# New h scaled sixteen rows behind its result, operand sums and row scales at other rows, and one more pair whose weights are added by POOL

## The chip, the cores and the metric

The kernel runs on one core of one Trainium2 chip. The metric is the device time of one execution, in microseconds. The core has five engines that each work through their own list of instructions in order: PE (matmuls), ACT and DVE (work on whole tiles of 128 partitions), POOL, and SP, which issues most transfers. POOL issues transfers too, among them those that add to what lies in the destination.

## The reference

Two layers over a hidden state h of 512 tokens by 2048 channels. Layer 0 is a hybrid of forgetting attention and an RWKV-7 time mix; layer 1 is a gated MLP with spatial gating. After each layer h is updated twice: once by the normed output of the layer, and once by a gated product of the per-layer inputs p. All is fp32. What matters here is the end of layer 0 and the beginning of layer 1:

```
for i in range(DEPTH):
    xn = rms_norm(h, norm_pre[i])
    ...                                   # layer 0: attention and time mix; layer 1:
    proj = xn @ c_w_in[j]
    u, v, g = _split(proj, (GMLP_W, GMLP_W, GMLP_W))
    oc = chunked_spatial_gating(u, v, c_ln_g[j], c_ln_b[j], c_w_s[j], c_b_s[j])
    y = (oc * jax.nn.silu(g)) @ c_w_out[j]
    ...
    h = h + rms_norm(y, norm_post[i])
    h = h + (p[i] @ ple_w_proj[i]) * jax.nn.sigmoid(h @ ple_w_gate[i])
```

The last line of layer 0 is the stage called the gate here (`first_gate`), and `xn @ c_w_in` of layer 1 is `layer_c`. The norm of layer 1 is split in two: the column factor `norm_pre` is multiplied onto the new h (line 1164), and the row factor, one over the root of the mean square of each token, comes later, from sums of squares.

## The kernel before, in words

**Products.** Each fp32 number is written as a high and a low part, and each product takes three matmuls (high by high, high by low, low by high). The large products, 512 by 2048 by 2048 and the like, are made by a Strassen-Winograd scheme: seven products of half size in place of eight, for a pair of column blocks of the weight. A `Pair` stands for 512 + 512 columns; `seven` (line 1547) runs the products in the order handed in. In the gate and in the first third of layer_c that order is for two pairs, a and b: b1 a1 b2 a2 a5 a6 a3 a4 a7 b5 b6 b3 b4 b7. The letters V, U and G of layer_c are the three thirds of `c_w_in`; its first product stage is over V[0] (a) and V[1] (b).

**Rows.** Each of the products has eight rows, one for each 128 input channels of the half. A row is one cast of a weight tile to its high part on ACT (line 1541, into `whi`), one subtraction on DVE that makes the low part (line 1542, `wlo`), and then PE's matmuls: 12 of 256 columns in the gate, 6 of 512 columns in layer_c. `whi` and `wlo` have four buffers each, so ACT and DVE can be four rows ahead of PE. If a pair is `whole`, each fifth row of weights uses a pair of extra buffers, `half0` and `half1`; otherwise those buffers take half tiles of the load for product 4.

**Weights.** Each product needs a sum or difference of weight blocks. Products 1, 2, 3 and 6 load blocks over SP's queue. Products 5 and 7 add a block by an accumulate transfer that POOL issues (`grow`, line 1489). Product 6 adds two tiles on DVE (line 1493). Product 4 depends on the pair: a `whole` pair adds by POOL's transfer, another loads two half tiles over SP's queue and adds each on DVE, again at line 1493.

**Operands.** The other side of each product, h, also enters as sums and differences of its quarters. In the names of the program `yh`, `xh`, `xl`, `yl`, `sq`, `sg` are tiles of 128 by 512 for such sums and their parts; a sum is made on DVE (lines 1413 and 1414), its high part by ACT (line 973), its low part by DVE (line 974). The steps `s1`, `s24`, `s3`, `x2`, `x22` make the operands of product 5 (s1), of 6 and 3 (s24), of 7 (s3) and of 2 and 4 (x2, x22); each has four parts q. `early(q)` copies a quarter of h as the operand of product 1 of the next stage.

**What sets the order.** `later(n, step)` notes a step n rows ahead; `tick` counts a row and runs the steps that are due (line 1469). The order on an engine then follows from the priority of an instruction, the place where it was written, and `high_priority`, which puts instructions ahead of others written earlier; a scheduler that builds the program fixes each engine's list from that. While it runs, nothing passes anything else on one engine.

**A result of the gate.** `emit` (lines 1142 to 1168) takes one result: a sigmoid on ACT, a multiplication and the addition to h on DVE (lines 1152 to 1154), the square on ACT (line 1155) and, on DVE, its sum into `accq` or `rstdB` (line 1157, which of them depends on the half e of the tokens). Line 1159 stores the new h from the `yh` tile over SP's queue to `hd` in DRAM, and the scale of line 1164 writes `yh` times `norm_pre` over the same tile, in two ACT instructions of 128 by 256. The scale has to wait until the store has read the tile. In the kernel before it is noted five rows behind the result. After the last product `self.clock += 100` runs all steps left over.

**Row factors.** `done` (line 1733) is called after each product of layer_c; after the first one it puts 16 matmuls with a tile of ones against `accq` and `rstdB` (line 1739), which add up the squares of each token and give the row factors.

Of the kernel before, what the change touches and what calls it, by code (L numbers as in the profile page):

```python
# [11 lines left out]
AF = mybir.ActivationFunctionType  # L12
# [4 lines left out]
P = 128  # L17
# [89 lines left out]
class Net:  # L107
# [986 lines left out]
    def first_gate(self, H, state, wp, ps):  # L1094
        nc, i = self.nc, self.i
        s, update, s1, s24, s3, x22 = state
        npre = self.cols["norm_pre"]
# [5 lines left out]
        def late(q):  # L1103
            update(q, 1)
            update(q + 4, 1)
            s1(q)

        def fetch(tiles, *which):
# [18 lines left out]
        cs, x2 = C[0], C[2]  # L1127

        def early(q):
            if q == 0:  # L1130
                cs[1] = self.whole_set()
            self.put(cs[1], q, H[q, 0])

        steps = [((1, 6, 19, 28)[q], lambda q=q: late(q)) for q in range(4)]
        steps += [((11, 15, 33, 37)[q], lambda q=q: s24(q)) for q in range(4)]
        steps += [((23, 26, 43, 45)[q], lambda q=q: s3(q)) for q in range(4)]
# [5 lines left out]
        steps += [(90, lambda: fetch([self.slot("xl", k, F32) for k in range(4)], (6, 1), (7, 1), (4, 1), (5, 1)))]  # L1142
        steps += [(103 + q, lambda q=q: x2(q)) for q in range(4)]
        steps += [(107 + q, lambda q=q: early(q)) for q in range(4)]
        for n, step in sorted(steps, key=lambda x: x[0]):
            self.later(n, step)

        def emit(pr, m, n, src):
# [12 lines left out]
            def scaled():  # L1161
                for a in range(2):
                    c = 16 + 2 * q + a
                    nc.scalar.activation(H[q, e][:, a, :], H[q, e][:, a, :], AF.Copy, scale=npre[:, c : c + 1])

            self.later(5, scaled)

        W = i["ple_w_gate"][0]
        self.seven(FIRST(*[Pair(W, 2 * j * T, 2 * j, emit) for j in range(2)]), Sets(s), ps, fm=True)
        self.clock += 100  # L1170
        self.tick()
        s1, s24, s3, x22 = C[3:]
        steps = [(2 + 3 * q, lambda q=q: s1(q)) for q in range(4)]
        steps += [(14 + 4 * q, lambda q=q: s24(q)) for q in range(4)]
        steps += [(30 + 2 * q, lambda q=q: s3(q)) for q in range(4)]
        steps += [(38 + 2 * q, lambda q=q: x22(q, True)) for q in range(4)]
        return accq, last["act"], cs, steps
# [435 lines left out]
    def layer_c(self, cp, sets, steps, accq, after, wp, ps):  # L1613
# [83 lines left out]
        G = [Pair(W, 2 * D + 2 * j * T, 2 * j, silu) for j in range(2)]  # L1697
        for pr in V:
            pr.whole = False
        order = FIRST(*V)  # L1700
# [32 lines left out]
        def done(step):  # L1733
            if step == 0:
                pc = self.t(ps, [P, 4, 2], "mm")
                for m in range(4):
                    for a in range(2):
                        c = 256 * a + m % 2 * P
                        nc.tensor.matmul(
                            pc[:, m, :], accq[m // 2][:, c : c + P], self.ones[:, 0:2], start=(a == 0), stop=(a == 1)  # L1740
                        )
                self.row_rstd(pc, rc, after)
                bs = self.t(wp, [P, T], "sq")[0:KT, 0:P]
                nc.sync.dma_start(bs, i["c_b_s"][0])

                def turned():
                    pt = self.t(ps, [P, KT], "mm")
                    nc.tensor.transpose(pt, bs, self.ident[0:KT, 0:KT])
                    self.bsT = self.t(lp, [P, KT], "bsT")
                    nc.vector.tensor_copy(self.bsT, pt)  # L1750

                self.later(12, turned)
# [290 lines left out]
```

## Time and profile before

| | |
|---|---|
| median of 3 runs | 2242.57 us (2239.11 to 2243.87) |
| profiled execution | 2242.89 us, span 2241.2 us, mean granted clock 0.994 |
| casts of the gate | from 1175.6 us of the span |
| casts of layer_c | from 1375.2 us |
| scales of line 1164 | 1242.1 to 1409.1 us |
| adds of half tiles, line 1493 | 1442.7 to 1516.9 us |

Times inside the span are counted from its start. A row of the timeline gives the start, the length, the engine, the line, the operation and its tiles, and in brackets how long the engine had nothing to run before and what released it. A row of the windows gives for each engine the busy time in the window and, in brackets, its instructions, then the granted clock of PE (1.00 is full speed), the busy share of the DMA engines and the data rate.

### The profile page before, as it was taken

What the parts mean: (1) busy time and instruction counts of PE and PEld (TensorE: products, weight loads), DVE (VectorE), ACT (ScalarE), POOL (GpSimd) and SP (SyncE); (2) the same over time, 40 slices, a digit from 0 to 9 for tenths busy, and PEclk for the clock granted to TensorE, in tenths of its full rate; (3) what the DMA queues carried; (4) which work ended last, traced back from release to release, by engine and by line L of the source; (5) the groups of instructions that cost most, each with busy time, mean ns of one, the idle gap of its engine ahead of it and who ended that gap; (6) DMA issues with size and microseconds to landing.
All of it is one profiled execution on the core that took longest, in us unless ns stands there. A gap on an engine that the chain in (4) does not pass through costs nothing. (4 is left out here: it accounts for less than half of the span.)

```text
span 2241.2 us, 43473 instructions
## 1 busy us (share of the span) xinstructions
PE 2193.2 (98%) x16535; PEld 1879.1 (84%) x16535; DVE 1666.0 (74%) x3236; ACT 1352.8 (60%) x2764; POOL 295.2 (13%) x356
## 2 busy tenths in 40 slices
PE   8999999999999999999999999999999999999998
PEld 7878888888888788889999998777877878999887
DVE  8766667666634777787879867887677678978977
ACT  5545545555543677766567656655565567757754
POOL 2000010101000000000210111011121121120031
PEclk9999999999999999999999999999999999999999
DMA  7322222223223633326988878589779687688796
GB/s 236 92 79 67 77 77 79 79 68 86 77 81 101 212 94 104 99 80 199 197 228 234 185 188 205 155 200 224 163 158 238 160 194 179 148 198 264 212 239 170
DMA packets 304208, 343.35 MB, mean 153 GB/s; under 512 B 15821, under 2 KB 188014, under 8 KB 302974
## 3 DMA queue, kind: packets, MB, share of 16 engines
q1 hardware_dynamic: 238590, 243.03, 34.8%
q0 software_dynamic: 43520, 83.90, 21.8%
q10 hardware_dynamic: 21888, 13.64, 2.2%
q8 instruction: 130, 2.13, 0.4%
q14 instruction: 80, 0.66, 0.1%
HBM read 305.61 MB, written 34.90 MB: 152 GB/s over the span
## 5 line engine op out<-in xcount | busy, mean ns | idle before, releaser
L1542 DVE TENSOR_TENSOR wlo<-rq,whi 128x512 fp32r<-128x512 f32 x494 | 336.6, 689 | 143.9 <-ACT whi L1541 138.1
L1541 ACT CAST whi<-rq 128x512 fp32r<-128x512 f32 x494 | 303.2, 620 | 191.9 <-PE mm L1577 131.6
L213 PE MATMUL mm<-xh,whi 128*128 128x512 f32 x992 | 412.2, 416 | 0.0
L215 PE MATMUL mm<-xh,wlo 128*128 128x512 f32 x992 | 392.1, 395 | 0.0
L214 PE MATMUL mm<-xl,whi 128*128 128x512 f32 x992 | 390.1, 393 | 0.0
L197 ACT CAST whi<-raw 128x512 fp32r<-128x512 f32 x272 | 167.5, 617 | 149.7 <-PE mm L214 103.0
L199 DVE TENSOR_TENSOR wlo<-raw,whi 128x512 fp32r<-128x512 f32 x272 | 186.0, 695 | 92.5 <-ACT whi L197 69.6
L215 PEld LDWEIGHTS mm<-xh,wlo 128*128 128x128 f32 x992 | 186.4, 188 | 40.9
L213 PEld LDWEIGHTS mm<-xh,whi 128*128 128x128 f32 x992 | 187.2, 189 | 33.1
L214 PEld LDWEIGHTS mm<-xl,whi 128*128 128x128 f32 x992 | 187.4, 189 | 29.6
L1577 PE MATMUL mm<-whi,yh 128*128 128x512 f32 x436 | 141.6, 395 | 4.1 <-DVE yh L974 2.8
L1577 PE MATMUL mm<-whi,yl 128*128 128x512 f32 x432 | 142.4, 397 | 0.2 <-ACT whi L1541 0.2
L1542 DVE TENSOR_TENSOR wlo<-raw,whi 128x512 fp32r<-128x512 f32 x157 | 107.4, 691 | 47.3 <-ACT whi L1541 45.8
L1577 PE MATMUL mm<-whi,xl 128*128 128x512 f32 x440 | 142.2, 392 | 0.0
L1541 ACT CAST whi<-raw 128x512 fp32r<-128x512 f32 x157 | 96.4, 619 | 70.2 <-PE mm L1577 51.5
L1577 PE MATMUL mm<-xh,whi 128*128 128x256 f32 x696 | 128.5, 286 | 3.2 <-ACT whi L1541 3.2
L1577 PEld LDWEIGHTS mm<-xh,whi 128*128 128x128 f32 x696 | 109.9, 194 | 3.5 <-ACT whi L1541 3.4
L1577 PE MATMUL mm<-xl,whi 128*128 128x256 f32 x520 | 99.0, 291 | 6.7 <-ACT xl L973 3.6
L1577 PEld LDWEIGHTS mm<-whi,yh 128*128 128x128 f32 x436 | 82.6, 190 | 21.9 <-DVE yh L974 3.2
L1577 PE MATMUL mm<-xh,wlo 128*128 128x256 f32 x348 | 99.5, 286 | 0.2 <-DVE wlo L1542 0.2
L1577 PEld LDWEIGHTS mm<-whi,yl 128*128 128x128 f32 x432 | 81.9, 190 | 18.0 <-ACT comb L1588 0.6
L1577 PEld LDWEIGHTS mm<-whi,xl 128*128 128x128 f32 x440 | 82.7, 188 | 17.0
(525 smaller groups left out, 5123.2 us busy)
## 6 DMA issues: line engine op xcount, KB each, us to landing
raw<-in_ab_w_in_dram SPq DMA_DIRECT2D x128, 512.0 KB, 3.9
rq<-in_c_w_in_dram POOLq DMA_DIRECT2D x52, 512.0 KB, 7.9
rq<-in_c_w_in_dram SPq DMA_DIRECT2D x50, 512.0 KB, 4.3
rq<-in_ple_w_gate_dram SPq DMA_DIRECT2D x44, 512.0 KB, 6.2
rq<-in_ple_w_gate_dram POOLq DMA_DIRECT2D x36, 512.0 KB, 8.3
raw<-in_c_w_in_dram SPq DMA_DIRECT2D x26, 512.0 KB, 6.4
rq<-in_c_w_out_dram SPq DMA_DIRECT2D x24, 512.0 KB, 5.1
rq<-in_ab_w_out_dram POOLq DMA_DIRECT2D x20, 512.0 KB, 7.4
```

The source lines that it names most:

```text
L197: nc.scalar.copy(hi[:, : m * n], src)
L199: self.weng.tensor_tensor(lo[:, : m * n], src, f(hi[:, : m * n]), ALU.subtract)
L213: nc.tensor.matmul(acc, hi, xhi[k], start=(k == 0), stop=False)
L214: nc.tensor.matmul(acc, hi, xlo[k], start=False, stop=False)
L215: nc.tensor.matmul(acc, lo, xhi[k], start=False, stop=(k == nk - 1))
L1541: self.cast = nc.scalar.copy(hi, src)
L1542: nc.vector.tensor_tensor(lo, src, f(hi), ALU.subtract)
L1577: nc.tensor.matmul(o, x, y, start=(first and r == 0 and j == 0 and not a), stop=(r == 7 and j == 2), **more)
```

## The change

Seven things are edited. In the gate: the sums `s24` are noted at rows 11, 15, 32, 35 and not at 11, 15, 33, 37, and they are written with a priority that puts them ahead of the results of the gate; `early` and `x2` of the next stage change places; the scale is noted sixteen rows behind its result, and each of its two instructions must stand behind the latest cast of weights; and the leftover steps are no longer run at the end of the stage, so that they fall due in the rows of layer_c. In layer_c: the operand sums are noted at other rows; V[0] is `whole` now, V[1] still isn't; and the 16 ones-matmuls come two rows behind the second product instead of right behind the first.

```diff
@@ first_gate @@
+        def first(q):
+            with tc.high_priority(150):
+                s24(q)
+
...
-        steps += [((11, 15, 33, 37)[q], lambda q=q: s24(q)) for q in range(4)]
+        steps += [((11, 15, 32, 35)[q], lambda q=q: first(q)) for q in range(4)]
...
-        steps += [(103 + q, lambda q=q: x2(q)) for q in range(4)]
-        steps += [(107 + q, lambda q=q: early(q)) for q in range(4)]
+        steps += [(103 + q, lambda q=q: early(q)) for q in range(4)]
+        steps += [(110 + 2 * q, lambda q=q: x2(q)) for q in range(4)]
...
             def scaled():
                 for a in range(2):
                     c = 16 + 2 * q + a
-                    nc.scalar.activation(H[q, e][:, a, :], H[q, e][:, a, :], AF.Copy, scale=npre[:, c : c + 1])
-
-            self.later(5, scaled)
+                    with tc.issue_after(self.cast.ins):
+                        nc.scalar.activation(H[q, e][:, a, :], H[q, e][:, a, :], AF.Copy, scale=npre[:, c : c + 1])
+
+            self.later(16, scaled)
...
-        self.clock += 100
-        self.tick()
         s1, s24, s3, x22 = C[3:]
-        steps = [(2 + 3 * q, lambda q=q: s1(q)) for q in range(4)]
-        steps += [(14 + 4 * q, lambda q=q: s24(q)) for q in range(4)]
-        steps += [(30 + 2 * q, lambda q=q: s3(q)) for q in range(4)]
-        steps += [(38 + 2 * q, lambda q=q: x22(q, True)) for q in range(4)]
+        steps = [(17 + 2 * q, lambda q=q: s1(q)) for q in range(4)]
+        steps += [(25 + 3 * q, lambda q=q: s24(q)) for q in range(4)]
+        steps += [(37 + 3 * q, lambda q=q: x22(q, True)) for q in range(4)]
+        steps += [(48 + 3 * q, lambda q=q: s3(q)) for q in range(4)]
@@ layer_c @@
-        for pr in V:
-            pr.whole = False
+        V[1].whole = False
...
-            if step == 0:
-                pc = self.t(ps, [P, 4, 2], "mm")
...
-                self.row_rstd(pc, rc, after)
+            if step == 1:
+
+                def row_scales():
+                    pc = self.t(ps, [P, 4, 2], "mm")
...
+                    self.row_rstd(pc, rc, after)
+
+                self.later(2, row_scales)
```

Lines of the changed kernel stand three to six lower: 1541 and 1542 become 1544 and 1545, 1164 becomes 1169, 1493 becomes 1496.

**First place: ACT in the gate, around the scale that stood before the operand cast `xl6`** (product 6 of pair a, S1 of the prediction). `whi` and `half0` are casts of weights, `xh`, `xl` are operands, `col89` the column of `norm_pre`. Before:

```order
L1541 CAST whi_3205_16200<-rq1_3078_15512 128x512
L1164 ACTIVATE yh2_2706_13403<-yh2_2706_13403,col89_72_254 128x256 x2
L1541 CAST half0_3207_16216<-rq1_3078_15512 128x512
L973 CAST xh0_3211_16250<-yh11_2960_14979 128x512
L973 CAST xh0_3211_16250<-yh13_2954_14957 128x512
L1541 CAST whi_3209_16234<-rq2_3183_16076 128x512
L973 CAST xh0_3211_16250<-yh15_2956_14965 128x512
L973 CAST xl6_3169_16008<-sq_3168_16006 128x512
L1541 CAST whi_3213_16252<-rq2_3183_16076 128x512
```

After:

```order
L1544 CAST half0_3207_16212<-rq1_3078_15512 128x512
L973 CAST xh0_3211_16250<-yh13_2954_14957 128x512
L1169 ACTIVATE yh0_2704_13397<-yh0_2704_13397,col89_72_254 128x256
L1544 CAST whi_3209_16234<-rq2_3183_16072 128x512
L1169 ACTIVATE yh0_2704_13397<-yh0_2704_13397,col89_72_254 128x256
L973 CAST xl6_3165_15971<-sq_3164_15969 128x512
L1544 CAST whi_3213_16252<-rq2_3183_16072 128x512
```

The scale of yh2 stood ahead of three casts of weights and of xl6. Now that of yh0 stands there, one instruction of it on each side of a cast of weights, and the scale of yh2 stands behind xl6.

**Second place: ACT in the gate, around the scales of yh4 and yh6** (S2). Before:

```order
L1541 CAST whi_3251_16545<-rq2_3183_16076 128x512
L1164 ACTIVATE yh4_2787_13893<-yh4_2787_13893,col89_72_254 128x256 x2
L1541 CAST whi_3253_16562<-rq3_3188_16111 128x512
L1541 CAST half0_3255_16578<-rq3_3188_16111 128x512
L1164 ACTIVATE yh6_2789_13900<-yh6_2789_13900,col89_72_254 128x256 x2
L1541 CAST whi_3257_16595<-rq4_3198_16158 128x512
L1541 CAST whi_3259_16611<-rq4_3198_16158 128x512
L1541 CAST whi_3261_16628<-rq5_3204_16197 128x512
```

After:

```order
L1544 CAST whi_3253_16558<-rq3_3188_16107 128x512
L1544 CAST half0_3255_16574<-rq3_3188_16107 128x512
L1544 CAST whi_3257_16591<-rq4_3198_16154 128x512
L1544 CAST whi_3259_16607<-rq4_3198_16154 128x512
L1544 CAST whi_3261_16624<-rq5_3204_16193 128x512
L1544 CAST whi_3263_16640<-rq5_3204_16193 128x512
L1169 ACTIVATE yh4_2787_13893<-yh4_2787_13893,col89_72_254 128x256 x2
L1169 ACTIVATE yh6_2789_13900<-yh6_2789_13900,col89_72_254 128x256
L1544 CAST half0_3271_16697<-raw_3270_16694 128x512
L1169 ACTIVATE yh6_2789_13900<-yh6_2789_13900,col89_72_254 128x256
```

Between the weights rq3 and rq4 stood the scale of yh6. Now four casts of rq4 and rq5 stand ahead of both scales.

**Third place: DVE in layer_c, ahead of product a4** (S5). `wlo` is the low part of a row of weights, `yh9` and so on are low parts of the operand of that product, which starts with the weights named rq2 in the last group of each piece; `raw` and `rq` are tiles of weights. Before, two pieces, first where the half tiles are added:

```order
L1493 TENSOR_TENSOR rq4_3441_17667<-rq4_3441_17667,half0_3619_18339 128x512
L1542 TENSOR_TENSOR wlo_3590_18198<-raw_3563_18091,whi_3589_18197 128x512
L1493 TENSOR_TENSOR rq4_3441_17667<-rq4_3441_17667,half1_3620_18342 128x512
L1633 BN_STATS bst_3388_17486<-xh3_3495_17848 128x6
L1542 TENSOR_TENSOR wlo_3592_18208<-raw_3563_18091,whi_3591_18207 128x512
```

and then where yh9 stands:

```order
L1542 TENSOR_TENSOR wlo_3610_18294<-rq2_3428_17617,whi_3609_18293 128x512
L1542 TENSOR_TENSOR wlo_3612_18304<-rq2_3428_17617,whi_3611_18303 128x512
L974 TENSOR_TENSOR yh3_3528_17966<-sq_3526_17963,yh2_3527_17965 128x512
L1542 TENSOR_TENSOR wlo_3616_18320<-rq3_3433_17639,whi_3615_18319 128x512
L1633 BN_STATS bst_3388_17486<-xh2_3529_17969 128x6 x2
L1542 TENSOR_TENSOR wlo_3618_18330<-rq3_3433_17639,whi_3617_18329 128x512
L1413 TENSOR_TENSOR sq_3536_17999<-yh4_2787_13893,yh5_2827_14176 128x512
L1413 TENSOR_TENSOR sq_3543_18026<-yh6_2789_13900,yh7_2828_14182 128x512
L974 TENSOR_TENSOR yh9_3552_18056<-sg_3550_18053,yh8_3551_18055 128x512
```

After:

```order
L1545 TENSOR_TENSOR wlo_3594_18236<-rq0_3564_18119,whi_3593_18235 128x512
L974 TENSOR_TENSOR xl15_3529_17984<-sg_3527_17981,xl14_3528_17983 128x512
L1545 TENSOR_TENSOR wlo_3599_18252<-rq1_3572_18148,whi_3598_18251 128x512
L974 TENSOR_TENSOR yh9_3538_18022<-sg_3536_18019,yh8_3537_18021 128x512
L1545 TENSOR_TENSOR half1_3601_18262<-rq1_3572_18148,half0_3600_18261 128x512
L1596 TENSOR_TENSOR comb_3437_17673<-mm_3549_18065,comb_3437_17673 128x512
L1545 TENSOR_TENSOR wlo_3605_18283<-rq2_3417_17577,whi_3604_18282 128x512
L974 TENSOR_TENSOR yh11_3547_18059<-sg_3545_18056,yh10_3546_18058 128x512
L1545 TENSOR_TENSOR wlo_3610_18299<-rq2_3417_17577,whi_3609_18298 128x512
```

The adds into rq2 to rq5 by half tiles are gone from V[0], and yh9 stands ahead of the first row of its product; before it stood behind the fourth.

More of the change, by code (lines that the diff above doesn't have):

```diff
@@ L1094, in first_gate @@
     def first_gate(self, H, state, wp, ps):
-        nc, i = self.nc, self.i
+        nc, tc, i = self.nc, self.tc, self.i
         s, update, s1, s24, s3, x22 = state
@@ L1733, in done @@
         def done(step):
-            if step == 0:
-                pc = self.t(ps, [P, 4, 2], "mm")
[L1736 to L1741, printed above, removed]
-                self.row_rstd(pc, rc, after)
+            if step == 1:
+                def row_scales():
+                    pc = self.t(ps, [P, 4, 2], "mm")
+                    for m in range(4):
+                        for a in range(2):
+                            c = 256 * a + m % 2 * P
+                            nc.tensor.matmul(
+                                pc[:, m, :], accq[m // 2][:, c : c + P], self.ones[:, 0:2], start=(a == 0), stop=(a == 1)
+                            )
+                    self.row_rstd(pc, rc, after)
+                self.later(2, row_scales)
                 bs = self.t(wp, [P, T], "sq")[0:KT, 0:P]
```

## The prediction

> **What bounds the kernel now.** I read the page first, then the span in windows of 20 us, then the timelines of the engines at the windows that fall short.
>
> ```profile
> span 2241.2 us, 43473 instructions
> PE 2193.2 (98%) x16535; PEld 1879.1 (84%) x16535; DVE 1666.0 (74%) x3236; ACT 1352.8 (60%) x2764; POOL 295.2 (13%) x356
> ```
>
> TensorE (PE) is busy for 98% of the span, so no edit outside PE pays except where PE stands or runs at a low clock. The windows show where that is inside the two stages that the diff touches (columns: window, length, PE, PEld, DVE, ACT, POOL busy, granted clock, DMA share, GB/s):
>
> ```profile
> 1240.00:1260.00 20.00, 20.00 (x169) 20.00 (x168) 18.09 (x26) 12.97 (x26) 1.20 (x1) 1.00 0.59 186
> 1260.00:1280.00 20.00, 16.12 (x113) 15.51 (x112) 15.86 (x27) 12.54 (x24) 6.74 (x6) 0.83 0.96 162
> 1300.00:1320.00 20.00, 16.59 (x123) 16.18 (x123) 11.26 (x17) 7.77 (x15) 1.20 (x1) 0.91 0.74 199
> 1340.00:1360.00 20.00, 16.83 (x120) 15.97 (x119) 12.47 (x20) 11.41 (x22) 3.64 (x3) 0.91 0.93 183
> 1400.00:1420.00 20.00, 15.29 (x61) 12.25 (x60) 13.07 (x22) 11.81 (x24) 1.49 (x2) 0.83 0.71 174
> 1420.00:1440.00 20.00, 20.00 (x90) 16.54 (x89) 19.89 (x32) 15.70 (x26) 0.00 (x0) 1.00 0.60 185
> 1460.00:1480.00 20.00, 17.23 (x70) 13.74 (x69) 18.29 (x31) 13.22 (x24) 4.81 (x4) 0.91 0.88 185
> 1520.00:1540.00 20.00, 18.38 (x80) 14.66 (x79) 13.28 (x23) 9.68 (x18) 2.44 (x2) 1.00 0.95 233
> ```
>
> An undisturbed window holds 169 matmuls of the gate (1240) or 90 of layer_c (1420). What a short window lost is therefore 20 us times the missing share: S1 (1260) 113 of 169, 6.6 us; S2 (1300) 5.4; S3 (1340) 5.8; S4 (1400) 61 of 90, 6.4; S5 (1460) 4.4; S6 (1520) 2.2; together 30.8 us. That is more than PE stood, because the granted clock falls below 1.00 in those windows too. These are the stalls that PE names:
>
> ```profile
> 1270.35 0.58 PE L1577 MATMUL mm<-xl,whi 128*128 128x256 f32 x1 [3.57 <-ACT xl L973]
> 1308.21 0.50 PE L1577 MATMUL mm<-xh,whi 128*128 128x256 f32 x2 [3.19 <-ACT whi L1541]
> 1344.84 0.51 PE L1577 MATMUL mm<-xl,whi 128*128 128x256 f32 x2 [1.18 <-ACT whi L1541]
> 1350.01 0.51 PE L1577 MATMUL mm<-xl,whi 128*128 128x256 f32 x2 [1.55 <-ACT whi L1541]
> 1407.53 1.87 PE L1739 MATMUL mm<-ones,rstdB 128*128 128x2 f32 x8 [4.71 <-DVE rstdB L1157]
> 1469.82 1.25 PE L1577 MATMUL mm<-whi,yh 128*128 128x512 f32 x3 [2.77 <-DVE yh L974]
> 1536.10 0.50 PE L1577 MATMUL mm<-whi,yh 128*128 128x512 f32 x1 [1.31 <-ACT whi L1541]
> ```
>
> In brackets: how long PE stood, and what released it. Five of the seven name ACT, which is 60% busy; so I looked at what ACT itself waited for just before:
>
> ```profile
> 1266.28 0.91 ACT L1164 ACTIVATE yh<-yh,col 128x256 f32<-128x256 f32 x2 [2.83 <-DMA hd<-yh]
> 1269.68 0.61 ACT L973 CAST xl<-sq 128x512 fp32r<-128x512 f32 x1
> 1306.75 0.91 ACT L1164 ACTIVATE yh<-yh,col 128x256 f32<-128x256 f32 x2 [6.57 <-DMA hd<-yh]
> 1340.00 0.91 ACT L1164 ACTIVATE yh<-yh,col 128x256 f32<-128x256 f32 x2 [4.16 <-DMA hd<-yh]
> 1343.37 0.91 ACT L1164 ACTIVATE yh<-yh,col 128x256 f32<-128x256 f32 x2 [1.95 <-DMA hd<-yh]
> 1348.55 0.91 ACT L1164 ACTIVATE yh<-yh,col 128x256 f32<-128x256 f32 x2 [2.72 <-DMA hd<-yh]
> 1405.24 0.91 ACT L1164 ACTIVATE yh<-yh,col 128x256 f32<-128x256 f32 x2 [3.94 <-DMA hd<-yh]
> 1406.06 0.61 ACT L1155 ACTIVATE sq<-yh 128x512 f32<-128x512 f32 x1
> 1534.91 0.62 ACT L1541 CAST half<-rq 128x512 fp32r<-128x512 f32 x1 [4.90 <-DMA rq<-in_c_w_in_dram]
> ```
>
> The first five gaps (S1 to S4) have one cause. ACT runs in order; the scale of line 1164 overwrites a half of h and must wait until its store has read it; the casts of weights and operands that PE needs stand behind it. The store is long under way because it shares the DMA engines:
>
> ```profile
> 1252.32 7.44 SPq L1159 DMA_DIRECT2D hd<-yh  x2
> 1294.36 0.53 SPq L1159 DMA_DIRECT2D hd<-yh  x1
> rq<-in_c_w_in_dram POOLq DMA_DIRECT2D x52, 512.0 KB, 7.9
> rq<-in_c_w_in_dram SPq DMA_DIRECT2D x50, 512.0 KB, 4.3
> L1164 ACT ACTIVATE yh<-yh,col x32: 491/506/511, 1242.1 to 1409.1; 128x256 f32<-128x256 f32 x32
> ```
>
> The store issued at 1294.36 released ACT only at 1306.75, 12.4 us later; the second of the two that run from 1252.32 to 1259.76 released it at 1266.28, some 6.9 after its issue.
>
> **The change part by part.** The rows of the changed order were counted by the weight cast at which an instruction stands (one cast per row of weights; 20 us hold 169/12 rows of the gate, 1.42 us each, and 90/6 of layer_c, 1.33 us each). No arithmetic is added: 32 scales of 0.51 us, the same sums, and 16 ones-matmuls stay; only places move, and product 4 of V[0] changes its way of adding.
>
> *S1, scales sixteen rows behind and sums first.* The sums now push the results of yh0 and yh2 back, and with them their stores. The cast that PE lacked (xl6, ended 1270.29, wanted at 1270.35 - 3.57 = 1266.78) no longer stands behind the scale of yh2, but behind that of yh0, whose store I place at about 1260.4, a row later than yh2's was. Its landing is open: 6.9 us as for its neighbour gives 1267.3, and then a scale, a cast and xl6, 2.1 us of ACT, leave PE 2.6 us short; a store that is through in half that time leaves it short of nothing. Loss and wait stand as 6.6 to 3.6, so the residual is 0 to 4.8 us. The gain lies between 0 (the store later still) and 6.6; I take 4, the middle of 6.6 and the 1.8 that the neighbour's landing leaves.
>
> *S2.* The scales of yh4 and yh6 now stand behind the casts of four more rows. PE came to the first of these at 1308.21 - 3.19 = 1305.0 and needs 4 x 1.42 = 5.7 us for them, so it wants the next at 1310.7; the store lands at 1306.75, and the two scales and a cast take 1.5. The stall goes: 5.4 at most, 3 if the store becomes 5 us later; I take 5. What hides the scales now is these four casts; without them the old 5.4 return.
>
> *S3.* In the order, the scales of yh7, yh1 and yh3 go back by about one cast only, and the next cast of weights still stands behind that of yh3. It waits for yh3's landing, 1348.55, as now. Two gaps (1.18 and 1.55) become one of some 3; I take 0, between a loss of 0.5 and a gain of 2.8 (5.8 less 3).
>
> *S4 and the start of layer_c.* The scale of yh9 moves by one cast and is still ahead of the squares of yh11, on which the ones-matmuls wait through DVE:
>
> ```profile
> 1380.40 0.95 PE L1739 MATMUL mm<-ones,accq 128*128 128x2 f32 x8
> 1406.79 0.69 DVE L1157 TENSOR_TENSOR rstdB<-rstdB,sq 128x512 f32<-128x512 f32 x1
> 1380.09 0.68 DVE L974 TENSOR_TENSOR xh<-yh,xh 128x512 fp32r<-128x512 f32 x1
> 1469.08 0.68 DVE L974 TENSOR_TENSOR yh<-sg,yh 128x512 fp32r<-128x512 f32 x1
> L1493 DVE TENSOR_TENSOR rq<-rq,half x16: 676/692/696, 1442.7 to 1516.9; 128x512 f32<-128x512 f32 x16
> ```
>
> But PE takes these 16 ones-matmuls behind ten more matmuls of 0.22 us, 2.2 us, and the eight on accq (0.95) now run inside the gap: 4.71 becomes about 1.6. Against it stands a wait that is new: at 1380 the eight were the cover of xh1, ready at 1380.77; two DVE instructions of 0.69 are now ahead of it, 1382.2, and PE is there at 1380.4, 1.8 us. Idle falls by 4.71 - 1.6 - 1.8 = 1.3. I take 1.5, between -1 (the new gap brings a low clock) and 3.5.
>
> *S5, product 4 of V[0].* DVE set this stall: it worked 19.89 and 18.29 us of the windows at 1420 and 1460, and gave the yh that PE lacked at 1469.76. Eight of the 16 adds of line 1493 (8 x 0.692 = 5.5 us) leave it, and the sum that PE waited for stands four rows further forward. That is more than the 2.77 us that PE stood, so up to 4.4 come back. In their place POOL issues four accumulate loads, each 7.9 to land; POOL was busy for 4.81 us of that window, and the rows want them from about 1462. I take 3.5, between 1 (a load late) and 4.4.
>
> A rule speaks against this part. In the Trainium skill, DMA: Bandwidth & Descriptors, SWDGE vs HWDGE vs iDMA, adding while loading is possible only on GpSimd's software queue, and inside each engine software and hardware queues are served in turn. The trace agrees in direction (7.9 us for POOL's loads, 4.3 for SP's, 12.4 for the store): by it each of the four new loads lengthens SP's loads that run beside it. The sum here holds nothing for that; the third rival does.
>
> *S6* is the half cast that waits for its load (4.90). Its place in ACT's order is the same: 0, between -1.5 and 1.5. The operand sums of layer_c only move within slack: DVE has some 7 us free of 20 at 1400 and 1520.
>
> The sum: 4 + 5 + 0 + 1.5 + 3.5 + 0 = 14 us off the profiled execution's 2242.9 (span 2241.2 and 1.7 around it; 0.3 above the median of the runs), **2229**.
>
> **The rivals.** *A, all waits on stores vanish*, as sixteen rows (23 us) against landings of 7 to 12 would have it: 6.6 + 5.4 + 5.8 + 6.4 - 0.9 at 1380 + 4.4 = 27.7, 2215. Against it: the order puts yh3's and yh9's scales one cast later, not sixteen; that the change does not do there what it says is in my sum already. *B, the waits move on*: the later results of yh0 make S1's new wait as long as the old, and the two gaps of S4 cost what one did; 5 of S2 and 2 of S5 remain, 2236. For it: DVE and ACT keep all their work, and loads still fill the engines (0.96 of the DMA at 1260). *C, slower*: V[0]'s rows now use the half buffers, every fifth cast, seven such casts, and the two earliest are put ahead of their turn as the one of S6 is. If each waits for its load as that did, with ACT in order behind it, each costs between S6's 2.2 and 2.6 (its 1.62 us of gap at S5's rate of 4.4 to 2.77): 15 to 18 us, all of the gain and more, 2244 to 2247, with some 2 more where POOL's new loads are late: up to 2249. It decides once ACT waits longer at them than the four casts ahead cover, 5.3 us. Against it: S6 is the one such wait in the trace, at a DMA share of 0.95, and at 1420 it is 0.60. *D, gaps without a low clock*: only the gaps above 3 us (3.19, 3.57, 4.71) brought the low clock, so S3's one gap of 3 costs 3 (2.8 more), S1's rest of some 1 its idle alone (0.9 more), and 2225 follows. Against it: the windows of the gaps of 1.55 and 2.77 have 0.91 as well. The Trainium skill, TensorE: Matmul & The Clock Gate, What's actually happening, has a rule that points this way: an idle window of about 3.4 us sets the half clock. This trace does not bear that out as a bound on a single gap.
>
> **How the numbers follow.** My forecast has 0.56, its own range 2224 to 2235 (half the distance of the terms' bounds). A has 0.07, B 0.22 (2234 to 2240), C 0.10, D 0.05. The time is that of the likeliest, 2229. From 2220 to 2241 leaves out A and most of C. What a measurement of this kernel tells from no change is about 0.2%, 4.5 us: faster is below 2238.1, slower above 2247.1. Faster are the forecast, A, D and two thirds of B: 0.83; the same the rest of B and half of C: 0.12; slower the other half of C: 0.05.
>
> **What would show it.** S2 right: PE undisturbed from 1295 to 1320, four casts of weights ahead of line 1164's successor. S1: a gap under 3 us before xl6, with the scale of yh0 waiting on its store. S3 and S4: scales that still wait 2 us or more, one gap of about 3 us near 1345, and a new one of about 1.8 near 1370 at the first rows of layer_c. S5: DVE under 19 us of 20 at 1420 to 1460 and no gap on a yh. C shows as ACT waits on DMA at half casts of 4 us and more. Wrong would be the forecast if the 20-us windows of these stages lose more than 20 us in all, or if a window outside them changes.

## The result, and the profile after

The changed kernel takes 2228.89 us, median of 4 runs (2225.56 to 2231.20), beside 2241.79 (2239.11 to 2243.87) for the kernel before: a ratio of 0.9942, 95% interval 0.9923 to 0.9961. The forecast was 2229. The profiled execution took 2231.20, 11.7 less than that of before.

The page of the changed kernel, and its 20-us windows (columns as before):

```profile
span 2229.5 us, 43456 instructions
PE 2191.7 (98%) x16535; PEld 1876.3 (84%) x16535; DVE 1660.8 (74%) x3228; ACT 1355.4 (61%) x2764; POOL 311.6 (14%) x360
```

```profile
1260.00:1280.00 20.00, 17.20 (x130) 16.80 (x129) 15.42 (x26) 13.13 (x25) 6.12 (x6) 0.91 0.97 175
1300.00:1320.00 20.00, 20.00 (x169) 20.00 (x168) 15.21 (x22) 10.32 (x19) 1.50 (x2) 1.00 0.65 179
1320.00:1340.00 20.00, 18.72 (x152) 18.11 (x150) 14.63 (x25) 12.43 (x25) 6.92 (x6) 1.00 1.01 208
1340.00:1360.00 20.00, 15.60 (x103) 14.96 (x104) 13.00 (x21) 9.73 (x19) 2.41 (x2) 0.83 0.80 183
1400.00:1420.00 20.00, 19.04 (x90) 15.32 (x89) 16.18 (x26) 17.68 (x32) 2.55 (x1) 1.00 0.75 220
1460.00:1480.00 20.00, 20.00 (x89) 16.54 (x89) 16.35 (x26) 10.80 (x19) 4.88 (x4) 1.00 0.97 246
1520.00:1540.00 20.00, 18.50 (x74) 14.56 (x73) 9.66 (x15) 8.32 (x14) 1.93 (x2) 0.91 0.63 204
```

S2 (1300) and S5 (1460) have full windows now, S4 (1400) nearly. S1 (1260) is about a third gone: 39 matmuls of 169 are missing and not 56. S3 lies on both sides of 1340 and is worse than it was: 152 and 103 matmuls of 169, where one window with 120 was short. The stalls on PE, from its timeline:

```profile
1269.38 0.38 PE L1580 MATMUL mm<-xl,whi 128*128 128x256 f32 x1 [2.17 <-ACT xl L973]
1270.39 0.58 PE L1580 MATMUL mm<-xl,whi 128*128 128x256 f32 x1 [0.63 <-DVE xl L974]
...
1340.07 0.51 PE L1580 MATMUL mm<-xl,half 128*128 128x256 f32 x2 [0.85 <-ACT half L1544]
...
1346.37 0.80 PE L1580 MATMUL mm<-xl,whi 128*128 128x256 f32 x2 [4.11 <-ACT whi L1544]
...
1377.90 0.96 PE L1580 MATMUL mm<-whi,xh 128*128 128x512 f32 x3 [0.27 <-DVE xh L974]
...
1403.30 1.05 PE L1743 MATMUL mm<-ones,rstdB 128*128 128x2 f32 x8 [0.74 <-DVE rstdB L1161]
...
1524.19 0.50 PE L1580 MATMUL mm<-whi,yh 128*128 128x512 f32 x1 [1.20 <-ACT whi L1544]
```

and the scales on ACT that stand before them, with the scale's row of the waits between 1160 and 1560 us (total, times, longest), first of the changed kernel and then of the kernel before:

```profile
1267.39 0.51 ACT L1169 ACTIVATE yh<-yh,col 128x256 f32<-128x256 f32 x1 [3.25 <-DMA hd<-yh]
...
1335.57 0.91 ACT L1169 ACTIVATE yh<-yh,col 128x256 f32<-128x256 f32 x2 [3.84 <-DMA hd<-yh]
...
1339.00 0.51 ACT L1169 ACTIVATE yh<-yh,col 128x256 f32<-128x256 f32 x1 [1.48 <-DMA hd<-yh]
...
1345.30 0.51 ACT L1169 ACTIVATE yh<-yh,col 128x256 f32<-128x256 f32 x1 [4.86 <-DMA hd<-yh]
...
1400.61 0.91 ACT L1169 ACTIVATE yh<-yh,col 128x256 f32<-128x256 f32 x2 [3.48 <-DMA hd<-yh]
```

```profile
ACT yh L1169 <- DMA hd<-yh: 18.8, 6, 4.9
```

```profile
ACT yh L1164 <- DMA hd<-yh: 30.4, 13, 6.6
```

To put a number on each stall without counting windows, the matmuls of both kernels can be paired: PE has the same list in both, apart from the ones-matmuls and a few between 1394 and 1491 us that change places, so the n-th matmul of one is the n-th of the other. How much earlier it starts than in the kernel before is the lead; what a stall gave or took is the lead behind it less the lead ahead of it. For all kernels that ran (us, each from one profiled execution; the medians are of all runs):

| kernel | ahead of S1 | behind S1 | behind S2 | behind S3 | behind S4 | behind S5 | behind S6 | end | median |
|---|---|---|---|---|---|---|---|---|---|
| changed kernel | -0.6 | 1.4 | 6.8 | 2.9 | 8.3 | 12.7 | 10.3 | 11.8 | 2228.89 |
| e1_scale5 | -0.1 | 0.4 | 0.5 | 1.5 | 7.6 | 11.3 | 12.9 | 11.3 | 2232.52 |
| e2_v0_halves | 1.5 | 3.9 | 9.3 | 3.6 | 9.6 | 11.5 | 9.7 | 9.9 | 2234.37 |
| e3_no_priority | -0.9 | 5.8 | 11.2 | 6.7 | 12.1 | 16.4 | 18.0 | 19.2 | 2226.87 |
| e4_scale24a | -1.1 | 5.6 | 11.0 | 9.5 | 11.7 | 16.8 | 18.3 | 20.3 | 2222.69 |
| e5_before_prio | -2.6 | -2.5 | -3.5 | -4.8 | -5.4 | -5.4 | -5.1 | -2.4 | 2245.37 |
| e6_ones_step0 | 0.1 | 2.3 | 7.7 | 2.4 | 8.3 | 11.9 | 12.9 | 15.1 | 2230.93 |
| e7_fetch100 | -1.8 | 1.9 | 7.3 | 2.7 | 7.9 | 12.3 | 13.3 | 10.0 | 2231.60 |
| e8_best5 | 1.7 | 8.1 | 13.5 | 19.3 | 18.8 | 23.9 | 23.8 | 25.4 | 2220.37 |
| e9_small_grow | -0.5 | 1.4 | 6.8 | 12.6 | 14.8 | 19.9 | 21.8 | 22.3 | 2220.73 |
| e10_double_qd | 0.0 | 0.9 | 6.3 | 0.5 | 6.0 | 10.4 | 8.4 | 9.2 | 2234.31 |
| e11_cand32 | -0.6 | 6.0 | 11.4 | 17.2 | 20.9 | 26.0 | 26.5 | 26.8 | 2216.17 |
| e12_before_v0 | -1.7 | -1.3 | -2.2 | -1.0 | -1.0 | 4.4 | 4.8 | 4.8 | 2235.19 |

So the changed kernel gained 2.0 at S1, 5.4 at S2, lost 3.9 at S3, gained 5.4 at S4 with the beginning of layer_c, 4.4 at S5, lost 2.4 at and ahead of S6, and gained 1.5 behind these stages; with the 0.6 that it was behind at first, 11.8. The total came out near the forecast; its terms for S1, S3, S4 and S6 did not. The runs of one kernel spread by 2 to 10 us, so the medians carry differences of some 4 us and the stall sizes come from the leads. A lead is that of one execution: how far one can be trusted is seen at e7_fetch100, where the same list of work ran a second time.

### The profile page after: what moved, and what is told of

It reads as the page before. It is cut to its first block, busy times and chain, and to the rows that moved or that the text cites. A ratio compares the mean times of both kernels' runs of the same rounds, so it can differ in the third digit from the quotient of the medians.

```text
span 2229.5 us, 43456 instructions
## 1 busy us (share of the span) xinstructions
PE 2191.7 (98%) x16535; PEld 1876.3 (84%) x16535; DVE 1660.8 (74%) x3228; ACT 1355.4 (61%) x2764; POOL 311.6 (14%) x360
## 5 line engine op out<-in xcount | busy, mean ns | idle before, releaser
L1545 DVE TENSOR_TENSOR wlo<-rq,whi 128x512 fp32r<-128x512 f32 x485 | 330.6, 688 | 138.4 <-ACT whi L1544 135.3
L1544 ACT CAST whi<-rq 128x512 fp32r<-128x512 f32 x485 | 298.4, 621 | 189.5 <-PE mm L1580 121.4
L1545 DVE TENSOR_TENSOR half<-rq,half 128x512 fp32r<-128x512 f32 x111 | 76.4, 688 | 34.2 <-ACT half L1544 34.1
L1492 POOL DMA_DIRECT2D rq<-in_c_w_in_dram x56 | 67.6, 1220 | 242.3 <-DVE wlo L1545 162.2
L1544 ACT CAST half<-rq 128x512 fp32r<-128x512 f32 x111 | 69.0, 621 | 45.9 <-PE mm L1580 27.7
```

The source lines that it names most:

```text
L1492: nc.gpsimd.dma_start(view(tl), block(*where), accum_op=ALU.add)
L1544: self.cast = nc.scalar.copy(hi, src)
L1545: nc.vector.tensor_tensor(lo, src, f(hi), ALU.subtract)
```

## The experiments

The theory at this point: the waits of scales on stores are what counts, each edit acts on one stall, and S3 and the rest of S1 are left.

**The scale put back to five rows.**

```diff
-            self.later(16, scaled)
+            self.later(5, scaled)
```

> The changed kernel with one number put back: the scale noted 5 rows behind its result, not 16. Theory (stalls at S1 to S4 come from scales that wait on stores ahead of casts): the gap of 3 us at about 1300 (S2) returns with its 5.4 us; S3 stays as long as it is (its three scales stand at most one or two casts earlier); S1 is as in the changed kernel, since the scales of yh0 and yh2 stand at the same casts. So 2229 + 5 = 2234, of which S2 is nearly all. Rival (S2 went because of the sums put first): S2 stays gone and the time is 2229.

2232.52, ratio to the kernel before 0.9952 (0.9940 to 0.9964). From its timelines of PE and ACT:

```profile
1307.72 0.51 PE L1580 MATMUL mm<-xh,whi 128*128 128x256 f32 x2 [3.13 <-ACT whi L1544]
```

```profile
1306.26 0.91 ACT L1169 ACTIVATE yh<-yh,col 128x256 f32<-128x256 f32 x2 [8.09 <-DMA hd<-yh]
```

S2 is back in the place and at the length of before, behind the same scale: the lead moves by 0.1 there instead of 5.4. The theory holds for S2. It was wrong in two things. S1 was not as in the changed kernel: its gap is 3.73 us there and not 2.17, and the lead gained 0.5 and not 2.0. And S3 did not stay; with five rows it gained 1.0 where the changed kernel lost 3.9, so sixteen rows made S3 worse in these executions. That is one reason why the time rose by 3.6 and not by 5.

**V[0] back to half tiles.**

```diff
-        V[1].whole = False
+        for pr in V:
+            pr.whole = False
```

> The changed kernel with V[0] adding its product 4 by half tiles on DVE as before. Theory: eight adds of 0.69 us are on DVE again between 1430 and 1470, product a4 waits some 2 to 3 us for its operands, 3 to 4.4 us lost: 2232 to 2233. Rival (the new due times of the operand sums alone mended S5): no gap above 1 us there, 2229. Rival (the half buffers and POOL's loads cost something): faster than 2229, and the rest gap at about 1524 smaller.

2234.37, ratio 0.9960 (0.9947 to 0.9972), 5.5 above the changed kernel, more than expected. Its timeline of PE has

```profile
1442.62 0.97 PE L1580 MATMUL mm<-whi,xl 128*128 128x512 f32 x3 [1.22 <-DVE xl L974]
```

and smaller gaps of 0.6 to 0.7 before and after it; no single gap of 2 us, but from behind S4 to behind S5 it gained 1.9 and the changed kernel 4.4. So 1.9 of S5 come with the adds still on DVE (by the new due times, as I read it; no run tries them alone), and the adds cost the rest. In the profiled executions 2.5 us are this edit; S3, which it does not touch, lost 5.7 here and 3.9 there, and the rest of the 5.5 lies within the spread of the runs.

**V[0] alone on the kernel before**, the same edit the other way.

> The kernel before with one edit alone: V[0] whole, so that POOL's transfers do the addition of its product 4 and each fifth of its rows is cast into the half buffers; the due times of the operand sums are the old ones. Theory (S5 was DVE with 5.5 us of work too much): the gap of 2.8 us at 1470 goes or falls below 0.7 us, 3 to 4.4 us gained, 2238 to 2240. Rival (POOL's loads land late, or half casts that wait for loads stop ACT): ACT waits of 3 us or more on loads in layer_c, 2242 or above. Rival (the new due times mended S5, not this): the gap stays above 2 us, 2241 to 2244.

2235.19, ratio 0.9963 (0.9949 to 0.9977), less than the 2238 to 2240 expected; the profiled execution took 2238.10. PE has no gap above 0.3 us between 1408 and 1531, and its window at S5 is full:

```profile
1460.00:1480.00 20.00, 20.00 (x90) 16.57 (x89) 18.45 (x31) 13.22 (x23) 5.31 (x5) 1.00 0.98 221
```

The lead moves from -1.0 to 4.4 at S5, 5.4. Taking DVE's eight adds away is enough to end S5, without the new due times. POOL's four loads had landed by 1468.2, ahead of need. The half cast of S6 waits 4.5 us for its load, as it did (4.9); of all the other half casts of layer_c up to 1560 one waits for a load, 0.7 us. That refutes the first rival, and the second too: the gap went without the new due times.

**The sums without priority.**

```diff
         def first(q):
-            with tc.high_priority(150):
-                s24(q)
+            s24(q)
...
-        steps += [((11, 15, 32, 35)[q], lambda q=q: first(q)) for q in range(4)]
+        steps += [((11, 15, 33, 37)[q], lambda q=q: first(q)) for q in range(4)]
```

> The changed kernel with the sums s24 written at their old rows and without priority. In its order the results of yh0 and yh2 stand eight and three casts earlier than in the changed kernel, their stores are issued earlier, but one instruction of yh2's scale stands ahead of the operand cast xl6. Theory (what counts is when the store before xl6 has landed): yh2's store lands at about 1266 as before, the stall at S1 stays between 2 and 5 us of loss, time 2227 to 2231. Rival (the sums put first are what halved S1): the old 6.6 us return, 2231 to 2232.

2226.87, ratio 0.9926 (0.9914 to 0.9937). Both expectations fell: S1 is not there at all.

```profile
1260.00:1280.00 20.00, 20.00 (x168) 19.96 (x167) 19.84 (x34) 14.92 (x28) 7.69 (x7) 1.00 1.11 200
```

```profile
1263.92 0.91 ACT L1168 ACTIVATE yh<-yh,col 128x256 f32<-128x256 f32 x2
1265.24 0.51 ACT L1168 ACTIVATE yh<-yh,col 128x256 f32<-128x256 f32 x1
```

The stores are issued at 1251.2 and 1258.3 (in the changed kernel both at 1261 to 1262.3), and the scales ahead of xl6 wait for nothing. I had taken yh2's store to land at 1266 as before; its scale's first half found it landed by 1265.24. So the sixteen rows, not the priority, would have ended S1, and the priority brought 4.7 us of it back (a gain of 6.7 here, 2.0 there; 3.0 of it by the second execution of the changed kernel's list, e7_fetch100). Five rows with the priority gained 0.5 (e1_scale5).

**The priority alone on the kernel before.**

> The kernel before with the first edit alone: sums s24 at rows 11, 15, 32, 35 with priority. The run without priority showed S1 gone altogether and the time 2 us lower. Theory (the priority pushes the results of yh0 and yh2, and so their stores, behind the sums, to about 1261, and the scale of yh0 then waits ahead of xl6): the gap at S1 is as long as before, 2 to 4 us, all other stalls of the kernel before stay, time 2240 to 2245. Rival (the priority is worth something of its own in the kernel before): S1 below 1 us, 2234 to 2238.

2245.37, ratio 1.0010 (1.0000 to 1.0021). The theory holds:

```profile
1272.76 0.58 PE L1581 MATMUL mm<-xl,whi 128*128 128x256 f32 x1 [3.54 <-ACT xl L973]
```

```profile
1270.77 0.51 ACT L1168 ACTIVATE yh<-yh,col 128x256 f32<-128x256 f32 x1 [3.07 <-DMA hd<-yh]
```

The gap is as long as before (3.57), now behind the scale of yh0. This edit is worth nothing in the kernel before, or a little less.

**The scales of pair a at 24 rows.**

```diff
-            self.later(16, scaled)
+            self.later(24 if n < 2 else 16, scaled)
```

> The changed kernel with the scales of pair a (yh0 to yh7) noted 24 rows behind their results, those of pair b still 16. In its order xl6 and the casts of product b6 then stand ahead of these scales. Theory: the gaps at S1 (2.2 and 0.6 us) and S3 (0.8 and 4.1 us) go, and with them 4.6 and some 8 to 10 us: 2215 to 2219. Rival (loads of weights that are late with the stores keep PE waiting): S3 keeps a gap of 2 us or more, 2222 to 2226. Rival (the waits move on into layer_c): S1 and S3 go and other gaps of 3 us or more appear after 1360, 2226 to 2230.

2222.69, ratio 0.9909 (0.9896 to 0.9922): the first rival. S1 is gone (6.7 gained), S3 is down to a loss of 1.5, but one gap stays:

```profile
1346.89 0.80 PE L1580 MATMUL mm<-xh,whi 128*128 128x256 f32 x2 [4.25 <-ACT whi L1544]
```

```profile
1345.82 0.51 ACT L1169 ACTIVATE yh<-yh,col 128x256 f32<-128x256 f32 x1 [9.17 <-DMA hd<-yh]
```

The scale of yh3 was sent five casts further back, and still waited 9.2 us: its store, issued at 1329.8, took 16.0. So eight rows more were taken up by a slower store, and the question became what makes that store slow. The DMA queues of the changed kernel between 1320 and 1346, as shares of 16 engines' time, gave two candidates, POOL's queue (q0) and SP's (q1):

```profile
q0 software_dynamic: 1632, 3.15, 69.9%
q1 hardware_dynamic: 2176, 2.10, 26.6%
```

**The loads of SP's queue moved back** (`xl<-qd`, from row 90 to row 100).

```diff
-        steps += [(90, lambda: fetch([self.slot("xl", k, F32) for k in range(4)], (6, 1), (7, 1), (4, 1), (5, 1)))]
+        steps += [(100, lambda: fetch([self.slot("xl", k, F32) for k in range(4)], (6, 1), (7, 1), (4, 1), (5, 1)))]
```

> The changed kernel with the four loads xl<-qd (1 MB over SP's queue) noted at row 100 of the gate and not 90. The longest stall left is S3: the store of yh3 was issued at 1332.2 and released its scale at 1345.3, 13.1 us, while the DMA engines were busy to 1.01 of their time. Theory (the store waits for what shares the engines, and the loads stand ahead of it in SP's queue): released within 10 us, the gap of 4.1 us falls below 2, time 2222 to 2226. Rival (POOL's accumulate loads alone set the landing): 12 us or more, S3 unchanged, 2229. Rival (the loads then come late for their own results): a new gap near 1365, 2228 to 2232.

2231.60, ratio 0.9951 (0.9934 to 0.9969). It tells nothing on the question, because the edit did not move the loads; on SP's queue they stand where they did, ahead of the store of yh3 (changed kernel: 1323.72 and 1327.80):

```profile
1323.17 0.95 SPq L1115 DMA_DIRECT2D xl<-qd  x2
1326.54 1.56 SPq L1163 DMA_DIRECT2D hd<-yh  x2
1328.20 1.40 SPq L1115 DMA_DIRECT2D xl<-qd  x2
1332.56 0.36 SPq L1163 DMA_DIRECT2D hd<-yh  x1
```

The run is of use in another way. Up to 1600 us the timelines of all five engines have the same work in the same order as in the changed kernel, so this is a second execution of it. S2, S4 and S5 gained 5.4, 5.2 and 4.4 here and 5.4, 5.4 and 4.4 there; S3 lost 4.6 and 3.9. But S1 gained 3.7 here and 2.0 there, and S6 gained 1.0 here and lost 2.4 there. These two cannot be read to better than some 2 or 3 us from one execution; the last section says why.

**POOL's loads cut short.** The eight accumulate loads of products b4 and b7 move an eighth of their bytes.

```diff
         def grow(tl, *where):
-            nc.gpsimd.dma_start(view(tl), block(*where), accum_op=ALU.add)
+            w = 64 if pr.cut and prod in (4, 7) else T
+            nc.gpsimd.dma_start(view(tl)[:, :, 0:w], block(*where)[:, :, 0:w], accum_op=ALU.add)
```

> The changed kernel in which the eight accumulate loads of POOL for products b4 and b7 of the gate move 64 of 512 columns (3.5 MB less between about 1318 and 1360; it leaves out seven eighths of the addition of these weight blocks). It measures what the store of yh3 waits for. Theory (POOL's accumulate loads fill the DMA engines and the store shares them): the store, 13.1 us in the changed kernel, releases its scale within 7 us, ACT does not stand at yh3 for more than 1 us, and the gap of 4.1 us is gone: 2218 to 2223. Rival (the store waits in SP's own queue behind the loads xl<-qd): 10 us or more, gap above 2 us.

2220.73 in one run. The scales of yh7, yh1 and yh3 wait for nothing, and the two windows of S3 are full:

```profile
1334.45 0.91 ACT L1169 ACTIVATE yh<-yh,col 128x256 f32<-128x256 f32 x2
1335.77 0.51 ACT L1169 ACTIVATE yh<-yh,col 128x256 f32<-128x256 f32 x1
```

```profile
1320.00:1340.00 20.00, 20.00 (x169) 20.00 (x169) 18.97 (x32) 16.03 (x32) 9.44 (x8) 1.00 0.59 129
1340.00:1360.00 20.00, 20.00 (x169) 20.00 (x168) 14.20 (x22) 12.59 (x23) 0.00 (x0) 1.00 0.66 191
```

The last two instructions here are the scale of yh3 (the first row ends with one of them, at 1334.86). Its store, issued at 1332.24, was through by then, 2.6 us at most, with the same loads in SP's queue ahead of it. That is shown, by one execution with a large effect: POOL's accumulate loads make the store of S3 slow.

**The loads of SP's queue doubled.**

```diff
+                for _ in range(2):
+                    nc.sync.dma_start(pj[q, e], self.qd[:, 2 * q : 2 * q + 2, e * 256 : e * 256 + 256])
```

> The changed kernel with each of the four loads xl<-qd issued twice, 1 MB more on SP's queue, a part of it ahead of the store of yh3. Theory (POOL's loads set the landing and SP's own bytes count little): the store releases its scale after 13 to 15 us and the gap stays between 4 and 7 us. Rival (SP's own queue sets it): 16 us or more, gap 7 us or more, 2233 or above.

2234.31 in one run. The store, issued at 1334.1, released its scale at 1348.24, 14.1 us, no more than in other kernels with the loads single (13.1 to 16.0 in the lower rows of the table below). The gap is longer than the theory had it:

```profile
1349.30 0.79 PE L1586 MATMUL mm<-xl,whi 128*128 128x256 f32 x2 [8.75 <-ACT whi L1550]
```

The landing speaks for the theory, the gap for the rival. What SP's queue adds is the later issue: six loads, not four, stand ahead of the store in SP's list, and it went out 1.9 us later. Against the changed kernel S3 lost 1.9 more; but e2_v0_halves, with the loads single, lost as much (5.7), so the gap alone does not tell what the doubled loads cost.

**The ones-matmuls right behind the first product.**

```diff
-            if step == 1:
+            if step == 0:
...
-                self.later(2, row_scales)
+                row_scales()
```

> The changed kernel with the 16 ones-matmuls right behind the first product of layer_c again. In its order the scales of yh15 and yh9 then stand behind the squares of yh11. Theory (S4 shrank from 4.7 to 0.7 us because PE has ten more matmuls to do before it needs the sums of squares): the gap returns, less than in the kernel before since ACT does not stand at yh9 first: 1 to 3 us, a new gap behind the scales is possible, 2229 to 2232. Rival (S4 shrank because stores land sooner): gap below 0.7, 2227 to 2229.

2230.93, ratio 0.9952 (0.9935 to 0.9968). No gap returned:

```profile
1400.02 1.05 PE L1743 MATMUL mm<-ones,rstdB 128*128 128x2 f32 x8
```

S4 gained 5.9 here and 5.4 in the changed kernel. The rival has the gap and the theory the time, but neither for its reason: in this order the squares of yh11 stand ahead of the scale of yh9, so ACT does not stand at a store before them. The edit moved two things, and so does not tell what ten matmuls of delay are worth alone.

**Two candidates.** Both leave the priority out; the scales of yh0 to yh6 come 24 rows behind, those of yh1 to yh7 40 or 32, and the ones-matmuls five rows behind the second product.

```diff
-            self.later(16, scaled)
+            self.later((24 if m < 2 else 32) if n < 2 else 16, scaled)
...
-                self.later(2, row_scales)
+                self.later(5, row_scales)
```

> A candidate: the changed kernel without priority on the sums (rows 33 and 37 as before), the scales of pair a 24 rows behind for yh0 to yh6 and 40 rows behind for yh1 to yh7 (in its order at the first casts of layer_c), and the ones-matmuls five rows behind the second product. Theory (S3 is a scale that waits on its store, wherever the store is slow): S1 and S3 are gone, S4 below 0.5 us: 2212 to 2217. Rival (S3 moves on, as it did with 24 rows, to other work that waits on the loads): a gap of 2 us or more between 1340 and 1400, 2219 to 2224.

> A candidate: the changed kernel without priority on the sums (old rows), the scales of yh0 to yh6 24 rows behind and those of yh1 to yh7 32 rows behind, that is at casts 216 to 219 and so ahead of the first rows of layer_c, and the ones-matmuls five rows behind the second product. Theory (the gap of 2.2 us at 1363 in the run with 40 rows is DVE and ACT catching up on late scales at the first rows of layer_c): that gap is below 1 us, S1 and S3 stay gone, 2215 to 2219. Rival (the stores have not landed at cast 216 either): a gap of 2 us or more at about 1355, 2220 to 2224.

With 40 rows 2220.37, ratio 0.9903 (0.9888 to 0.9919), as the rival had it: S1 and S3 are gone (6.4 and 5.8 gained), and 3.1 us are lost at the first rows of layer_c, where the scales now fall (the lead goes from 19.3 to 16.2 there):

```profile
1363.40 0.96 PE L1579 MATMUL mm<-whi,xh 128*128 128x512 f32 x3 [2.17 <-DVE xh L974]
```

With 32 rows 2216.17, ratio 0.9888 (0.9869 to 0.9907), as the theory had it, and the lowest of all, though its interval overlaps that of 40 rows: about 12 us below the changed kernel. That gap is 0.26 us, and the waits of the scales between 1160 and 1560 are down to one:

```profile
ACT yh L1168 <- DMA hd<-yh: 3.4, 1, 3.4
```

## Why the prediction was right

The time, the sign and the bound were right: PE stood at scales that wait for stores and at an overloaded DVE, and easing both gave nearly what was summed, 14 forecast and 11.7 (profiled executions) to 12.9 (medians) measured. The parts are less good than the sum.

- **S2**: 5 forecast, 5.4 measured, and e1_scale5 shows the step: with the scales back at five rows the stall is back in full, so it is the four casts ahead of the scales that end it.
- **S5**: 3.5 forecast, 4.4 measured; e12_before_v0 shows that taking the adds away is enough (5.4). One sign that I had set did not come: DVE did not fall under 19 us of 20 at 1420 to 1460.

```profile
1420.00:1440.00 20.00, 20.00 (x90) 16.54 (x89) 20.00 (x32) 12.66 (x22) 12.76 (x4) 1.00 0.45 116
1440.00:1460.00 20.00, 19.64 (x85) 15.51 (x85) 19.93 (x34) 15.96 (x29) 6.77 (x6) 1.00 1.11 205
```

  With 20.00 and 19.93 us (third engine column) DVE is as full as before (19.89 and 19.87), and PE stands for 0.36 us at an xl and not at a yh. So the busy share was no measure of the stall. Rival C's mechanism did not come: of the half casts of layer_c only that of S6 waited more than 0.4 us for its load, 4.8 us, as it had (4.9).
- **S1**: 4 forecast, 2.0 measured, inside the bounds. The failed step is the middle between two landings. The neighbour's landing of 6.9 us was the row at hand, it gave a wait of 2.6 and a gain of 1.8; measured were 6.4 us (1261.0 to 1267.4), gaps of 2.2 and 0.6, and 2.0. The second execution (e7_fetch100) had a landing of 6.1 us and gaps of 1.9 and 0.6, and gained 3.7, near the forecast; but that is the clock, which stayed at 1.00 there, and not a store through in half the time. And the edit that I read with the sixteen rows as one change was two, against each other (e3_no_priority, e5_before_prio).
- **S3**: 0 forecast, with -0.5 as the worst; -3.9 measured. The failed step is "It waits for yh3's landing, 1348.55, as now". The landing is not a fixed point: the store took 10.9 us before and 13.1 after. That POOL's loads make it slow is shown (e9_small_grow). Why they do so more in the changed kernel is read from when the next accumulate load goes out behind the store. In the changed kernel these are

```profile
1332.16 0.36 SPq L1163 DMA_DIRECT2D hd<-yh  x1
1338.01 1.20 POOL L1492 DMA_DIRECT2D rq<-in_ple_w_gate_dram  x1 [4.98 <-DVE wlo L1545]
```

  and for all kernels in which the scale waited for this store:

| kernel | store of yh3 issued | next accumulate load behind it, us | store through after, us |
|---|---|---|---|
| e1_scale5 | 1337.1 | 9.2 | 11.4 |
| e12_before_v0 | 1339.8 | 9.2 | 11.2 |
| before | 1337.6 | 8.2 | 10.9 |
| e5_before_prio | 1341.1 | 7.2 | 11.3 |
| changed kernel | 1332.2 | 5.9 | 13.1 |
| e3_no_priority | 1327.6 | 5.3 | 14.1 |
| e6_ones_step0 | 1333.2 | 4.8 | 13.8 |
| e2_v0_halves | 1331.6 | 4.5 | 13.7 |
| e7_fetch100 | 1332.6 | 2.6 | 13.5 |
| e10_double_qd | 1334.1 | 1.7 | 14.1 |
| e4_scale24a | 1329.8 | 1.5 | 16.0 |

  A cast that stands ahead of a scale lets its weight tile be freed earlier (POOL's load above waited for the subtraction, `wlo`), POOL's next load into that tile goes out earlier, and it shares the engines with the store on which the scale waits. The eleven kernels fall into two groups: 10.9 to 11.4 us where the next load came 7 us or more behind the store, 13.1 to 16.0 where it came earlier. Inside the second group the order is not clear (5.9 and 2.6 us went with 13.1 and 13.5), and the first group is also the four kernels in which S2's stall stands ahead of S3. No run held the loads back alone, so this last step is argued, not shown.
- **S4 and the start of layer_c**: 1.5 forecast, 5.4 measured, above the upper bound of 3.5. Two sizes failed. The new wait of 1.8 at the first rows of layer_c was 0.27. And I counted idle time alone, 1.3 us less, although my own table had S4 at 6.4 for a gap of 4.7: the shorter gap, 0.74, also spared the low clock (0.83 before in that window, 1.00 after). The 6.4 was low, too: eight of its 61 matmuls are ones-matmuls, which take 0.12 us each at full clock (0.95 for eight) and were counted as whole ones of 0.22; counted as they are, the window lost about 7.3. The wait of yh9's scale stayed as forecast, 3.48 us.
- **S6**: 0 forecast, bounds of 1.5; 2.4 lost from behind S5, of which 1.5 at the gap itself. The 1.5 gained behind these stages was in no term. In the second execution S6 gained 1.0 and the rest lost 3.3, so neither is shown to be the change's.

The misses at S3 (-3.9) and S4 (+3.9) cancel each other; that the total is so close is in part luck.

Of the rivals, A is refuted (18.8 us of waits on stores are left), and e11_cand32 shows what it would take. B (2234 to 2240) is refuted by the time. Of its mechanisms the later results of yh0 did keep a part of S1, S4 did not come, and S3, which grew, was not in it. The Trainium skill's rule on accumulate loads, which I left out of the sum and gave to rival C, did bear on this kernel, at S3 in the gate: DMA: Bandwidth & Descriptors, SWDGE vs HWDGE vs iDMA, has the engines serve software and hardware queues in turn. The traces agree in direction: the store of 256 KB took 2.6 us at most beside shortened loads and 13.1 beside whole ones. D could not be told from the forecast by the time; what the gaps show of it stands in the last section.

## What to carry to other kernels

When an engine that works in order stands at an instruction that waits for a transfer, putting it n rows later helps only where work that the bottleneck needs moves ahead of it; and the landing time is not a constant: loads that run beside the transfer slow it (shown here), and earlier casts may release such loads earlier (argued here). Take a stall's price from what its window lost, clock included, and not from the gap alone. Where two edits touch the same stall, price them apart before adding them; here one of them took back 3.0 to 4.7 of the 6.7 us that the other brought. Take a second execution of the same list before reading a part of 2 us from one.

## What the runs showed of the hardware

A gap of the same kind does not always cost the same. In e7_fetch100, which has the changed kernel's work in the same order, gaps of 1.90 and 0.62 us at S1 left the clock at 1.00 and 143 matmuls in the window; in the changed kernel 2.17 and 0.63 went with 0.91 and 130.

```profile
1260.00:1280.00 20.00, 17.47 (x143) 17.07 (x143) 17.08 (x29) 14.04 (x27) 7.23 (x6) 1.00 0.99 181
```

At S6 a gap of 1.31 went with 1.00 before, and one of 1.20 with 0.91 after. So neither a length of about 3 us (rival D) nor any other single length decides it in these traces. By the rule of the Trainium skill, TensorE: Matmul & The Clock Gate, What's actually happening, the activity windows run freely.

The traces agree, and how a gap falls across the windows fits what they show. In each trace the spells of low clock (0.5) begin on one grid of 3.41 us: in the kernel before at 1268.9, 1309.9, 1350.9, 1405.5 and 1470.3, which lie 12, 12, 16 and 19 steps apart, and each of the five lasts one or two steps. The steps at S1, first of the changed kernel, then of e7_fetch100 (columns as in the other windows, PE's busy time first, the clock third from the end):

```profile
1266.77:1270.18 3.41, 0.82 (x5) 0.42 (x3) 1.74 (x3) 2.79 (x7) 0.00 (x0) 1.00 1.09 190
1270.18:1273.60 3.42, 3.21 (x15) 3.21 (x16) 2.58 (x6) 2.66 (x6) 1.20 (x1) 0.51 0.55 81
```

```profile
1266.47:1269.88 3.41, 1.90 (x16) 1.69 (x15) 0.55 (x1) 1.60 (x4) 1.21 (x1) 1.00 1.13 220
1269.88:1273.29 3.41, 2.40 (x17) 2.20 (x18) 3.41 (x7) 3.41 (x8) 1.16 (x1) 1.00 0.84 148
1273.29:1276.70 3.41, 3.41 (x31) 3.41 (x30) 3.39 (x6) 2.56 (x5) 1.24 (x2) 1.00 0.78 112
```

In the changed kernel the gap fell almost whole into one step, and the next step had half the clock; in e7_fetch100 a border of the grid cut it in two, and the clock stayed. At S6 PE was busy for 2.20 us of 3.41 in the step that held most of the gap in the kernel before, with no low clock behind it, and for 1.91 in the changed kernel, with low clock. In the fourteen traces between 1255 and 1560, all 29 steps begun at full clock in which PE idled for over 45% were followed by low clock, and none of those under 38%. In between both occurred: the steps with 1.90 us at S1 of e7_fetch100 and 1.91 at S6 of the changed kernel, 44% idle, went different ways. This is read from the traces; no run moved a gap against the grid on purpose.
